# Sums of weight blocks made by adding DRAM-to-DRAM transfers, and 17 seven-product pairs for 13, in a hybrid encoder block

## The chip, the cores and the metric

The kernel runs on one core of a Trainium2 chip. The metric is the device time of one execution in microseconds. The time before is the median of three runs, 1146.89 us (1146.48 to 1147.50).

The core's engines are called by short names. PE is TensorE (matrix products; PEld is its loading of the stationary operand), DVE is VectorE, ACT is ScalarE, POOL or Pool is GpSimd, and SP is SyncE, which issues nearly all transfers. Sixteen DMA engines carry the transfers of all queues.

## The reference

One layer of an encoder block for 256 tokens of 2048 features, in float32:

```
hn   = rmsnorm(x);  proj = hn @ w_in            # (256, 2048) @ (2048, 3616)
mix  = concat(ssd_mixer(proj), pool_mixer(proj)) @ w_out
h    = x + rmsnorm(mix)
up   = rmsnorm(h) @ w_ffn_up                    # (256, 2048) @ (2048, 11264)
gate, val = split(up);  gate = gelu(dwconv3(gate))
ff   = (gate * val) @ w_ffn_down                # (256, 5632) @ (5632, 2048)
h    = h + rmsnorm(ff)
out  = h + rmsnorm(sigmoid(rmsnorm(h) @ w_ple_gate) * (p @ w_ple))
```

The change concerns the product with `w_ffn_down`, the down projection. The state-space mixer (`ssd_mixer`) matters because its small steps run on Pool.

## The kernel before

**Products.** Every float32 operand is split into a high part (rounded to float32r) and a low part (the rest), and a product is made of three: high by high, high by low, low by high. `split` (line 138) does this for weights: ACT casts the high part (line 147), DVE subtracts it (line 148). Every product is issued in `mm` (line 86), so all matrix products of the profile have the line L86 and are told apart by their tiles.

**Stages, in the order of the code.** Input projection of `dt` and the pooling inputs (`dtu`), then of the mixer's inputs in three slabs (`xbc`), then of `z` (tiles `z`); between them small steps of the mixer are put in by a list of jobs. Then the output projection (`wo`), the up product in 11 slabs of 512 gate and 512 value columns (`ga` and `va`), the down projection (`dn`), and the gate of the last embedding (`gt`). The mixer's steps on Pool that matter here: `rms` (lines 312 and 315) gives `rx`, the row scales with which DVE and ACT empty the first accumulators (lines 457 to 461); `seg_prep` (line 509) builds `ap` for the `seg` products; `weigh` (line 581) builds `w`; `far` (line 597) builds `xd` for the `yo` products, which stand among the products of `z`. In the up product Pool has one multiplication for each slab (line 767).

**Down projection.** `sublayer` (line 701) runs it in two halves of 1024 output columns. In each half `token_major` (line 240) walks through 22 pairs of weight rows: `raw` (line 151) loads a pair, 2 x 128 rows by 1024 columns (1024 KB), into one of three buffers. An ordinary pair is split and gives 24 products of 128 x 512. A fast pair goes through `seven_products` (line 201): it treats pair and column halves as a 2 x 2 matrix of blocks and needs seven block products in place of eight, 21 products in all. DVE makes the sums of weight blocks in place (lines 209 to 211), `hid_sums` (line 800) makes those of the input blocks, and `combine` (line 222) brings the accumulators together after the last fast pair. Fast are 6 of 22 pairs in the first half and 7 in the second (line 828). The input sums of the first four fast pairs are kept in two pages and used again in the second half.

**Buffers.** `page` (line 70) gives one of 13 buffers of 128 x 2048 float32; `mid` (line 73) one of three of half the size. During the up product all 13 pages are in use: six for `hid`, four for the normalised input (`wox`), two for `h`, one for `pl`.

**Order.** Each engine runs its queue strictly in the order of the built program, and an instruction waits there for the semaphores of its inputs. That order isn't the order of the code: a scheduler lays the instructions out when the program is built, by their priority, their dependencies and the buffers that are free. An instruction whose inputs are there and whose buffer is free can stand far ahead of its place in the code. Loads on SP are held by their buffers (`raw` has three), and where `load` (line 115) is told so also by the load before.

Of the kernel before, what the change touches and what calls it, by code (L numbers as in the profile page):

```python
# [51 lines left out]
def build(nc, a, out):  # L52
# [5 lines left out]
    with tile.TileContext(nc) as tc, \  # L58
            tc.tile_pool(name="const", bufs=1) as cp, \
            tc.tile_pool(name="weights", bufs=1) as wp, \  # L60
            tc.tile_pool(name="pages", bufs=1) as gp, \
            tc.tile_pool(name="small", bufs=1) as sp, \
            ExitStack() as early, \
            tc.tile_pool(name="pmain", bufs=6, space=bass.MemoryType.PSUM) as pm, \
            tc.tile_pool(name="pmisc", bufs=2, space=bass.MemoryType.PSUM) as pc:
# [44 lines left out]
        vt = cp.tile([P, V_N - V_SCW], F32, name="vt")  # L110
        small = ep.tile([P, 80 + 512], F32, name="small")

        last = {}

        def load(dst, src, ahead=False):

            with tc.issue_after(last["dma"]) if last and not ahead else nullcontext():
                return ins(nc.sync.dma_start(dst, src))
# [31 lines left out]

        def raw(name, src, a_, b_):
            r = wp.tile([P, 2048], F32, tag="raw", bufs=3, name=name)
            last["dma"] = load(r[:, :a_ * b_].rearrange("p (a b) -> p a b", a=a_), src, True)
            return r

# [42 lines left out]
                yield o, c  # L198
                c += o.shape[-1]

        def seven_products(name, r, a_, acc, alt, start, stop):

            v = r.rearrange("p (b c) -> p b c", b=4)
            b11 = split(f"{name}a", r[:, :512], 512)
            b2 = split(f"{name}b", r[:, 1024:], 1024)

            nc.vector.tensor_sub(v[:, 0:2], v[:, 1::2], v[:, 0:2])
            nc.vector.tensor_sub(v[:, 3], v[:, 3], v[:, 0])  # L210
            nc.vector.tensor_sub(v[:, 2], v[:, 2], v[:, 3])
            t13 = split(f"{name}c", r[:, :1024], 1024)
            t42 = split(f"{name}d", r[:, 1024:], 1024)
            for x, (wh, wl), c, o, own in (
                    ("a11", b11, 0, alt[0], True), ("a12", b2, 0, acc[0][0], False), ("s4", b2, 512, acc[0][1], False),
                    ("s1", t13, 0, alt[1], True), ("s3", t13, 512, alt[2], True), ("a22", t42, 0, acc[1][0], False),
                    ("s2", t42, 512, alt[3], True)):
                xh, xl = a_[x]
                for q, (xx, ww) in enumerate(((xh, wh), (xh, wl), (xl, wh))):
                    mm(o, xx, ww[:, c:c + 512], own and start and q == 0, own and stop and q == 2)  # L220

        def combine(name, acc, alt):

            m = [mid(f"{name}v{i}") for i in range(2)]
            p1, s16, s165, s167 = (m[i // 2][:, i % 2 * 512:(i % 2 + 1) * 512] for i in range(4))

            def add(o, a_, b):
                nc.vector.tensor_add(o, a_, b)

            nc.scalar.copy(p1, alt[0])  # L230
            add(s16, alt[3], p1)
            add(acc[0][0], acc[0][0], p1)
            add(s165, alt[1], s16)
            add(acc[0][1], acc[0][1], s165)
            add(s167, alt[2], s16)
            add(acc[1][0], acc[1][0], s167)
            add(s165, alt[2], s165)
            add(acc[1][1], acc[1][1], s165)

        def token_major(name, w, c0, ks, get, acc, tail=1, fast=(), alt=None, sums=None):  # L240


            group, nu = [], len(ks) // 2
            for u in range(nu):
                k0 = ks[2 * u]
                r = raw(f"{name}r{k0}", w[k0 * P:(k0 + 2) * P, c0:c0 + 1024]
                        .rearrange("(k p) c -> p k c", p=P), 2, 1024)
                if u in fast:
                    seven_products(f"{name}{k0}", r, sums(k0), acc, alt, u == fast[0], u == fast[-1])
                    continue  # L250
                for j in range(2):
                    group.append((k0 + j, *split(f"{name}{k0}_{j}", r[:, j * 1024:(j + 1) * 1024], 1024)))
                if nu - tail <= u < nu - 1:
                    continue

                order = [(t, o, g, q) for t in range(2) for o in columns(acc[t]) for g in group for q in range(3)] \
                    if u == nu - 1 or u - 1 in fast[-1:] else \
                    [(t, o, g, q) for g in group for t in range(2) for q in range(3) for o in columns(acc[t])]
                for t, (o, c), (k, wh, wl), q in order:
                    xh, xl = (v[:, t * P:(t + 1) * P] for v in get(k))  # L260
                    xx, ww = ((xh, wh), (xh, wl), (xl, wh))[q]
                    mm(o, xx, ww[:, c:c + o.shape[-1]], k == ks[0] and q == 0, k == ks[-1] and q == 2)
                if u - 1 in fast[-1:]:
                    combine(name, acc, alt)
                group = []
                aside()
# [464 lines left out]
        def ple(half):  # L731
            pl = page(f"pl{half}")
            acc = [main(f"ple{half}{t}") for t in range(2)]
            token_major(f"ple{half}", w_ple, half * 1024, [0, 1], lambda k: (pth[:, k, :], ptl[:, k, :]), acc)
            for t in range(2):
                for n in range(2):
                    nc.scalar.activation(pl[:, t * 1024 + n * 512:t * 1024 + (n + 1) * 512], acc[t][n],
                                         AF.Copy, scale=0.5)
            return pl
# [9 lines left out]
                      V_FN, Pairs)  # L749


        pl = [ple(0)]
        rf = row_rstd("rf", h)
        rfb = along_tokens("rfb", rf)
        hid = [page(f"hid{i}") for i in range(6)]
        for s in range(DFF // 512):
            sc = mid(f"gr{s}")
            for i in range(2):
                ga = main(f"ga{s}{i}")
                feature_pairs(f"ug{s}{i}", w_up, s * 512 + i * 256, hf, ga)  # L760
                o = sc[:, i * 512:(i + 1) * 512]
                total(o, ga)
                v = o.rearrange("p (f t) -> p f t", f=2)
                nc.vector.tensor_tensor(v, v, rfb.unsqueeze(1).to_broadcast([P, 2, L]), op=ALU.mult)
            cv = conv(f"fc{s}", sc, 3, V_FCW + 4 * s, NF, V_FCB + 4 * s)
            nc.scalar.activation(cv, cv, AF.Gelu_apprx_tanh)  # L766
            nc.gpsimd.tensor_tensor(cv.rearrange("p (f t) -> p f t", f=4), cv.rearrange("p (f t) -> p f t", f=4),  # L767
                                    rfb.unsqueeze(1).to_broadcast([P, 4, L]), op=ALU.mult)
            for i in range(2):
                va = main(f"va{s}{i}")  # L770
                feature_pairs(f"uv{s}{i}", w_up, DFF + s * 512 + i * 256, hf, va)
                c0 = (s % 2) * 1024 + i * 512
                hd = hid[s // 2][:, c0:c0 + 512]
                total(hd, va)
                nc.vector.tensor_mul(hd, hd, cv[:, i * 512:(i + 1) * 512])

        cur = {}

# [16 lines left out]
                hcache[k0], hcache[k0 + 1] = get_hid(k0), get_hid(k0 + 1)  # L795
            return hcache[k]

        keep, kept = [], {}

        def hid_sums(k):  # L800


            (h1, l1), (h2, l2) = get_hid(k), get_hid(k + 1)
            if k not in kept:
                src = hid[k // 8][:, (k % 8) * L:(k % 8 + 2) * L]
                a11, a21, a12, a22 = (src[:, i * P:(i + 1) * P] for i in range(4))
                n = len(kept)
                if n in (0, 2):
                    keep.append(page(f"hsum{k}", F32R))
                s = mid(f"hd{k}")  # L810
                s1, s2, s3, s4 = (s[:, i * P:(i + 1) * P] for i in range(4))
                nc.vector.tensor_add(s1, a21, a22)
                nc.vector.tensor_sub(s3, a11, a21)
                nc.vector.tensor_sub(s2, s1, a11)
                nc.vector.tensor_sub(s4, a12, s2)
                o = keep[-1][:, n % 2 * 1024:(n % 2 + 1) * 1024] if n < 4 else mid(f"he{k}", F32R)
                nc.scalar.copy(o[:, :512], s[:, :512])
                nc.vector.tensor_sub(o[:, 512:], s[:, :512], o[:, :512].bitcast(F32))
                if n < 4:
                    kept[k] = o  # L820
            else:
                o = kept[k]
            d = {f"s{i + 1}": (o[:, i * P:(i + 1) * P], o[:, 512 + i * P:512 + (i + 1) * P]) for i in range(4)}
            d.update(a11=(h1[:, :P], l1[:, :P]), a12=(h2[:, :P], l2[:, :P]), a22=(h2[:, P:], l2[:, P:]))
            return d

        hp = sublayer("dn", w_down, list(range(NF)), hid_get, gload("gffn", a["ffn_norm_post"][0]), h, V_PN,
                      fast=((2, 5, 8, 11, 14, 17), (2, 5, 8, 11, 14, 17, 19)), sums=hid_sums)


        pl.append(ple(1))
# [110 lines left out]
```

## Time and profile before

| what | us |
|---|---|
| median of three runs | 1146.89 |
| profiled execution, whole time | 1147.28 |
| profiled execution, span of the profile | 1145.5 |
| PE busy | 1126.3 |
| DVE busy | 824.8 |
| ACT busy | 598.3 |
| Pool busy | 122.5 |

The DMA engines moved 219 MB, nearly all on SP's queue (q1), and HBM was written with 2.1 MB. The granted clock of TensorE was 0.994 of full speed on average. In the profile a row of 40 digits divides the span into 40 slices of 28.6 us, each digit the busy share in tenths. A row of a timeline has start, duration, engine, line, operation, output and inputs, and in brackets the idle time before it and what ended it.

### The profile page before, as it was taken

The numbers are of one execution on the slowest core, as the hardware profiler recorded it, in microseconds if no ns is written. First come the engines' busy times: TensorE is split into PE (matmuls) and PEld (weight loads), VectorE is DVE, ScalarE is ACT, GpSimd is POOL, SyncE is SP. The second block draws the span as 40 slices with busy tenths as digits, with TensorE's granted clock in tenths as the row PEclk, the third lists the DMA queues.
The fourth block names the chain that finished last, engine by engine and source line by source line (L and its number), as shares of the span: only waits on it lengthen the run. The fifth ranks groups of instructions, "written<-read, shape, count | busy, mean of one in ns | idle before, by whom it ended". The sixth has DMA issues, their size and how long they took to land.

```text
span 1145.5 us, 15408 instructions
## 1 busy us (share of the span) xinstructions
PE 1126.3 (98%) x6057; PEld 971.6 (85%) x6057; DVE 824.8 (72%) x1060; ACT 598.3 (52%) x812; POOL 122.5 (11%) x123
## 2 busy tenths in 40 slices
PE   9998999999999999999999999999999999999996
PEld 9997987888888888888888888888888888887885
DVE  6578896654777665666766766668888888898573
ACT  7533543553675454544544545545555556657462
POOL 0274504200110000000000000000000000002001
PEclk9998999999999999999999999999999999999998
DMA  9952347546365555555555565556466646564752
GB/s 358 337 184 74 111 150 267 201 156 216 121 213 186 192 192 195 190 185 184 184 187 193 181 207 189 184 184 221 159 209 221 204 163 221 187 206 159 226 179 74
DMA packets 129592, 219.03 MB, mean 191 GB/s; under 512 B 3696, under 2 KB 96752, under 8 KB 128624
## 3 DMA queue, kind: packets, MB, share of 16 engines
q1 hardware_dynamic: 129232, 217.70, 57.4%
q8 instruction: 47, 0.77, 0.3%
q10 hardware_dynamic: 288, 0.36, 0.1%
q14 instruction: 25, 0.20, 0.1%
HBM read 215.95 MB, written 2.10 MB: 190 GB/s over the span
## 4 chain that ended last, share of the span: by engine, by line
PE 92%; DVE 5%; POOL 1%; ACT 1%; issue 1%; POOLq 0%; DVEq 0%; ACTq 0%
PE va L86 21%; PE ga L86 21%; PE dna L86 17%; PE woa L86 8%; PE gt L86 7%; PE dtu L86 4%; PE z L86 4%; PE xbc L86 3%; PE dns L86 3%; DVE cv L373 2%; DVE w L586 1%; DVE xb_0l L148 1%; PE ple L86 1%; PE yd L86 0%; DVE h L726 0%
## 5 line engine op out<-in xcount | busy, mean ns | idle before, releaser
L86 PE MATMUL ga<-wox,ug_0h 128*128 128x512 f32 x352 | 125.5, 395 | 0.0
L86 PE MATMUL ga<-wox,ug_1h 128*128 128x512 f32 x352 | 125.1, 394 | 0.0
L86 PE MATMUL va<-wox,uv_0h 128*128 128x512 f32 x352 | 124.8, 393 | 0.0
L86 PE MATMUL va<-wox,uv_1h 128*128 128x512 f32 x352 | 124.8, 393 | 0.0
L86 PE MATMUL ga<-wox,ug_0l 128*128 128x256 f32 x352 | 99.1, 282 | 0.0
L86 PE MATMUL ga<-wox,ug_1l 128*128 128x256 f32 x352 | 99.1, 282 | 0.0
L86 PE MATMUL va<-wox,uv_0l 128*128 128x256 f32 x352 | 99.1, 281 | 0.0
L86 PE MATMUL va<-wox,uv_1l 128*128 128x256 f32 x352 | 99.1, 281 | 0.0
L86 PEld LDWEIGHTS va<-wox,uv_0h 128*128 128x128 f32 x352 | 66.1, 188 | 15.0
L86 PEld LDWEIGHTS va<-wox,uv_1h 128*128 128x128 f32 x352 | 66.1, 188 | 15.0
L86 PEld LDWEIGHTS ga<-wox,ug_1h 128*128 128x128 f32 x352 | 66.1, 188 | 14.9
L86 PEld LDWEIGHTS ga<-wox,ug_0h 128*128 128x128 f32 x352 | 66.1, 188 | 14.8
L86 PE MATMUL dna<-dn_0h,hs 128*128 128x512 f32 x248 | 75.8, 393 | 0.0
L86 PE MATMUL dna<-dn_1h,hs 128*128 128x512 f32 x248 | 75.6, 393 | 0.0
L767 POOL TENSOR_TENSOR fc<-fc,rfb 128x1024 f32<-128x1024 f32 x11 | 26.4, 2404 | 440.2 <-ACT fc L766 440.2
L86 PEld LDWEIGHTS ga<-wox,ug_0l 128*128 128x128 f32 x352 | 66.2, 188 | 0.1
L86 PEld LDWEIGHTS ga<-wox,ug_1l 128*128 128x128 f32 x352 | 66.2, 188 | 0.0
L86 PEld LDWEIGHTS va<-wox,uv_0l 128*128 128x128 f32 x352 | 66.2, 188 | 0.0
L86 PEld LDWEIGHTS va<-wox,uv_1l 128*128 128x128 f32 x352 | 66.2, 188 | 0.0
L86 PEld LDWEIGHTS dna<-dn_1h,hs 128*128 128x128 f32 x248 | 46.5, 188 | 10.8
L86 PEld LDWEIGHTS dna<-dn_0h,hs 128*128 128x128 f32 x248 | 46.5, 188 | 10.7
L86 PE MATMUL dna<-dn_0l,hs 128*128 128x512 f32 x124 | 40.2, 393 | 0.0
(1075 smaller groups left out, 2860.3 us busy)
## 6 DMA issues: line engine op xcount, KB each, us to landing
dn0r<-w_ffn_down SPq DMA_DIRECT2D x22, 1024.0 KB, 5.5
dn1r<-w_ffn_down SPq DMA_DIRECT2D x22, 1024.0 KB, 5.5
zr<-w_in SPq DMA_DIRECT2D x8, 1024.0 KB, 5.2
wo0r<-w_out SPq DMA_DIRECT2D x8, 1024.0 KB, 5.6
wo1r<-w_out SPq DMA_DIRECT2D x8, 1024.0 KB, 5.5
gt0r<-w_ple_gate SPq DMA_DIRECT2D x8, 1024.0 KB, 6.0
gt1r<-w_ple_gate SPq DMA_DIRECT2D x8, 1024.0 KB, 5.6
dtur<-w_in SPq DMA_DIRECT2D x14, 528.0 KB, 8.6
```

The lines of the kernel that those rows point to most:

```text
L86: nc.tensor.matmul(o, lhsT, rhs, start=start, stop=stop, skip_group_check=True)
L148: last["dve"] = ins(nc.vector.tensor_sub(lo[:, s], src[:, s], hi[:, s].bitcast(F32)))
L373: nc.vector.scalar_tensor_tensor(o[:, lo:hi], i[:, lo + d:hi + d], vec(wcol + j * wstep + f), o[:, lo:hi], op0=ALU.mult, op1=ALU.add)
L586: nc.vector.scalar_tensor_tensor(w[:, h * P:(h + 1) * P], cbm[:, 0, g, t, :], dt[:, t, 8 * g + h:8 * g + h + 1], w[:, h * P:(h + 1) * P], ...
L767: nc.gpsimd.tensor_tensor(cv.rearrange("p (f t) -> p f t", f=4), cv.rearrange("p (f t) -> p f t", f=4), rfb.unsqueeze(1).to_broadcast([P, ...
```

## The change

The sums of weight blocks are no longer made by DVE. For each fast pair a DRAM tile of 128 x 2048 float32 is added, and Pool issues four transfers from DRAM to DRAM that fill it: a copy of the pair's four blocks (1024 KB); an adding transfer that adds the right-hand blocks to the first two (1024 KB); and two adding transfers within the tile (512 KB each). Each waits for the one before it. The code issues them in the loop of the up product, twice in each slab, four in one place for four different pairs. The signs of the sums change, and so `hid_sums` and `combine` change some additions to subtractions.

`seven_products` loads 768 KB of the unchanged blocks into a `raw` buffer with two transfers, and the 1024 KB of sums into a page with a third. The kept input sums and their two pages go, so `hid_sums` makes every pair's sums afresh. Fast pairs are now (2, 4, 7, 9, 12, 14, 17, 19) and (2, 4, 6, 8, 11, 13, 15, 17, 19): 17 for 13.

```diff
+        def block_sums(name, w, which):
+            jobs = []
+            def step(c0, k, i):
+                t = sums_[c0, k]
+                v = t.rearrange("p (b c) -> p b c", b=4)
+                if i == 0:
+                    nc.gpsimd.dma_start(t.rearrange("p (k c) -> p k c", k=2),
+                                        w[k * P:(k + 2) * P, c0:c0 + 1024].rearrange("(k p) c -> p k c", p=P))
+                elif i == 1:
+                    nc.gpsimd.dma_start(v[:, 0:2], w[k * P:(k + 2) * P, c0 + 512:c0 + 1024]
+                                        .rearrange("(k p) c -> p k c", p=P), accum_op=ALU.add)
+                elif i == 2:
+                    nc.gpsimd.dma_start(v[:, 3], v[:, 0], accum_op=ALU.add)
+                else:
+                    nc.gpsimd.dma_start(v[:, 2], v[:, 3], accum_op=ALU.add)
+            for c0, k in which:
+                sums_[c0, k] = dp.tile([P, 2048], F32, tag=f"bs{c0}_{k}", bufs=1, name=f"{name}{c0}_{k}")
+            for j in range(len(which) + 3):
+                jobs.append([lambda a_=(*which[j - i], i): step(*a_) for i in (3, 2, 1, 0) if 0 <= j - i < len(which)])
+            return jobs
...
-        def seven_products(name, r, a_, acc, alt, start, stop):
-            v = r.rearrange("p (b c) -> p b c", b=4)
+        def seven_products(name, w, k0, c0, a_, acc, alt, start, stop):
+            r = raw(f"{name}r", None, 0, 0)
+            last["dma"] = load(r[:, 512:1536], w[(k0 + 1) * P:(k0 + 2) * P, c0:c0 + 1024], True)
+            last["dma"] = load(r[:, :512], w[k0 * P:(k0 + 1) * P, c0:c0 + 512], True)
+            t = page(f"{name}t")
+            last["dma"] = load(t, sums_[c0, k0], True)
             b11 = split(f"{name}a", r[:, :512], 512)
-            b2 = split(f"{name}b", r[:, 1024:], 1024)
-            nc.vector.tensor_sub(v[:, 0:2], v[:, 1::2], v[:, 0:2])
-            nc.vector.tensor_sub(v[:, 3], v[:, 3], v[:, 0])
-            nc.vector.tensor_sub(v[:, 2], v[:, 2], v[:, 3])
-            t13 = split(f"{name}c", r[:, :1024], 1024)
-            t42 = split(f"{name}d", r[:, 1024:], 1024)
+            b2 = split(f"{name}b", r[:, 512:1536], 1024)
+            t13 = split(f"{name}c", t[:, :1024], 1024)
+            t42 = split(f"{name}d", t[:, 1024:], 1024)
...
+        dn_fast = (2, 4, 7, 9, 12, 14, 17, 19), (2, 4, 6, 8, 11, 13, 15, 17, 19)
+        ahead = block_sums("bs", w_down, [(c * 1024, 2 * u) for c, f in enumerate(dn_fast) for u in f])
...
+            for job_ in (ahead.pop(0) if ahead else ()):
+                job_()
             cv = conv(f"fc{s}", sc, 3, V_FCW + 4 * s, NF, V_FCB + 4 * s)
...
                 nc.vector.tensor_mul(hd, hd, cv[:, i * 512:(i + 1) * 512])
+            for job_ in (ahead.pop(0) if ahead else ()):
+                job_()
```

More of the change, by code (lines that the diff above doesn't have):

```diff
@@ L62, in build @@
             tc.tile_pool(name="small", bufs=1) as sp, \
+            tc.tile_pool(name="dram", bufs=1, space=bass.MemoryType.DRAM) as dp, \
             ExitStack() as early, \
@@ L111, in build @@
         small = ep.tile([P, 80 + 512], F32, name="small")
-        last = {}
+        last, sums_ = {}, {}
         def load(dst, src, ahead=False):
@@ L152, in raw @@
             r = wp.tile([P, 2048], F32, tag="raw", bufs=3, name=name)
+            if src is None:
+                return r
             last["dma"] = load(r[:, :a_ * b_].rearrange("p (a b) -> p a b", a=a_), src, True)
@@ L225, in combine @@
             p1, s16, s165, s167 = (m[i // 2][:, i % 2 * 512:(i % 2 + 1) * 512] for i in range(4))
-            def add(o, a_, b):
-                nc.vector.tensor_add(o, a_, b)
+            add, sub = nc.vector.tensor_add, nc.vector.tensor_sub
             nc.scalar.copy(p1, alt[0])
-            add(s16, alt[3], p1)
+            sub(s16, p1, alt[3])
             add(acc[0][0], acc[0][0], p1)
             add(s165, alt[1], s16)
-            add(acc[0][1], acc[0][1], s165)
+            sub(acc[0][1], acc[0][1], s165)
             add(s167, alt[2], s16)
@@ L237, in combine @@
             add(s165, alt[2], s165)
-            add(acc[1][1], acc[1][1], s165)
+            sub(acc[1][1], acc[1][1], s165)
         def token_major(name, w, c0, ks, get, acc, tail=1, fast=(), alt=None, sums=None):
@@ L245, in token_major @@
                 k0 = ks[2 * u]
+                if u in fast:
+                    seven_products(f"{name}{k0}", w, k0, c0, sums(k0), acc, alt, u == fast[0], u == fast[-1])
+                    continue
                 r = raw(f"{name}r{k0}", w[k0 * P:(k0 + 2) * P, c0:c0 + 1024]
                         .rearrange("(k p) c -> p k c", p=P), 2, 1024)
-                if u in fast:
-                    seven_products(f"{name}{k0}", r, sums(k0), acc, alt, u == fast[0], u == fast[-1])
-                    continue
                 for j in range(2):
@@ L796, in hid_get @@
             return hcache[k]
-        keep, kept = [], {}
         def hid_sums(k):
             (h1, l1), (h2, l2) = get_hid(k), get_hid(k + 1)
[L804 to L822, printed above, removed]
+            src = hid[k // 8][:, (k % 8) * L:(k % 8 + 2) * L]
+            a11, a21, a12, a22 = (src[:, i * P:(i + 1) * P] for i in range(4))
+            s, o = mid(f"hd{k}"), mid(f"he{k}", F32R)
+            s1, s2, s3, s4 = (s[:, i * P:(i + 1) * P] for i in range(4))
+            nc.vector.tensor_sub(s1, a22, a21)
+            nc.vector.tensor_sub(s3, a11, a21)
+            nc.vector.tensor_add(s2, s1, a11)
+            nc.vector.tensor_sub(s4, a12, s2)
+            nc.scalar.copy(o[:, :512], s[:, :512])
+            nc.vector.tensor_sub(o[:, 512:], s[:, :512], o[:, :512].bitcast(F32))
             d = {f"s{i + 1}": (o[:, i * P:(i + 1) * P], o[:, 512 + i * P:512 + (i + 1) * P]) for i in range(4)}
@@ L825, in hid_sums @@
             return d
+        assert not ahead
         hp = sublayer("dn", w_down, list(range(NF)), hid_get, gload("gffn", a["ffn_norm_post"][0]), h, V_PN,
-                      fast=((2, 5, 8, 11, 14, 17), (2, 5, 8, 11, 14, 17, 19)), sums=hid_sums)
+                      fast=dn_fast, sums=hid_sums)
         pl.append(ple(1))
```

## The prediction, made before the changed kernel ran

> **What bounds the kernel now.** I read the page's head first, then the busy time by stretch, then the chain that ended last, and last Pool's timeline, because the change puts its new work on Pool.
>
> ```profile
> span 1145.5 us, 15408 instructions
> PE 1126.3 (98%) x6057; PEld 971.6 (85%) x6057; DVE 824.8 (72%) x1060; ACT 598.3 (52%) x812; POOL 122.5 (11%) x123
> ...
> POOL 0274504200110000000000000000000000002001
> ...
> q1 hardware_dynamic: 129232, 217.70, 57.4%
> ```
>
> PE is busy nearly throughout, Pool (busy tenths in 40 slices) works mostly in the first quarter, and the DMA engines look nearly half free: SP's queue took 57.4% of them. The stretches say the same in numbers (columns: stretch, length, busy time of PE, PEld, DVE, ACT, POOL, clock, DMA share, GB/s):
>
> ```profile
> 0.00:57.30 57.30, 55.90 (x348) 55.11 (x349) 35.45 (x54) 37.25 (x54) 8.55 (x16) 1.00 0.93 348
> 57.30:172.00 114.70, 108.63 (x744) 100.82 (x744) 98.57 (x158) 48.39 (x67) 49.83 (x38) 0.97 0.40 130
> ...
> 805.00:1033.00 228.00, 228.00 (x989) 185.26 (x988) 197.83 (x234) 135.63 (x169) 0.90 (x2) 1.00 0.59 195
> ```
>
> In the down projection (the third row) PE has no gap at all, so only fewer products shorten it. In the first row the 16 DMA engines are full: 348 GB/s at a share of 0.93 is 374 GB/s for engines that are never idle, so that one pass over 1024 KB (1.049 MB) takes 2.80 us of all 16.
>
> **The products.** A pair of weight rows takes 24 products the ordinary way and 21 in `seven_products`. Four more pairs are fast, which is 12 products fewer. Their pace is in the chain:
>
> ```profile
> 849.06 11.11 PE dna L86 x48
> ```
>
> 11.11 / 48 = 0.231 us, and 12 x 0.231 = **2.8 us off**.
>
> The stage's loads and casts (the issues: count, KB of each, us to landing; then the group of a cast):
>
> ```profile
> dn0r<-w_ffn_down SPq DMA_DIRECT2D x22, 1024.0 KB, 5.5
> dn1r<-w_ffn_down SPq DMA_DIRECT2D x22, 1024.0 KB, 5.5
> ```
>
> ```profile
> L147 ACT CAST dn_1h<-dn1r 128x1024 fp32r<-128x1024 f32 x15 | 15.7, 1049 | 1.2 <-PE dna L86 1.2
> ```
>
> Beside these products and not on the path: DVE loses L209 to L211 in 13 pairs, and gains eight more sets of input sums (nothing is kept any more) and the casts of four more fast pairs. This lies under PE, which has no gap in 228 us while DVE is busy for 197.83. What SP loads grows from 44 times 1024 KB to 27 x 1 + 17 x 1.75 = 56.75 times: 12.75 x 2.80 = 36 us more of the DMA engines, 0.59 to 0.75 of the stage, hidden as well. The first load of sums takes a page that the up product gives back at its end; behind it stand the other SP loads. Two ordinary pairs (11.1 us of PE) cover its 5.5 us and four casts of 1.05 us; without that cover it would cost up to 9.7 us, once.
>
> **Where the transfers stand.** The code writes them between the slabs of the up product, but nothing there holds them: their inputs are weights in DRAM, and each sum has a buffer of its own. The scheduler decides, and the profile shows what it does with an instruction without inputs:
>
> ```profile
> 0.89 0.11 POOL half_up L841
> ```
>
> Line 841 stands behind the whole down projection, and it ran at 0.89 us. The built program of the changed kernel has Pool's queue so (position in the queue, new line numbers; A is the first pair, Z the last):
>
> ```
> 8    L213 copy A             11  L216 add A  [waits for copy A]
> 13   L219 add A [waits]      16  L221 add A  [waits]
> 32   L337 rx0m               55  L534 first ap
> 120  L219 add Z [waits]      121 L606 w
> 122  L221 add Z [waits]      125 L622 first xd
> ```
>
> All 68 transfers stand in positions 8 to 122, ahead of `xd` and interleaved with the small operations of the front. Each add waits on Pool for the transfer before it, and whatever is behind it in the queue waits too. In the kernel before, these operations ran at:
>
> ```profile
> 38.03 0.19 POOL L312 TENSOR_SCALAR rx0m<-rxq 128x1 f32<-128x1 f32 x1 [5.11 <-ACT rxj L338]
> 64.54 1.07 POOL L509 TENSOR_TENSOR ap<-dah,small 128x512 fp32r<-128x512 f32 x1 [20.71 <-DVE dah L484]
> 177.38 1.96 POOL L597 TENSOR_TENSOR xd<-xs,dec 128x1024 f32<-128x1024 f32 x1 [33.27 <-ACT xs L565]
> 186.50 1.02 PE L86 MATMUL yo<-xd,cbm 128*128 128x512 f32 x2
> ```
>
> PE needs them in its own fixed order: the first accumulators are emptied with `rx` (and are wanted for the next product), the `seg` products read `ap`, and `yo` at 186.5 reads `xd`. So PE stops at each until Pool is there, and the time at which Pool reaches `xd` moves everything behind it. PE's lost clock after such stops costs nothing more: Pool stays behind, not PE.
>
> **The price.** No adding transfer and no copy from DRAM to DRAM is in this trace. Per pair there are four: 1024 KB copied, 1024 KB added, twice 512 KB added. In units of one pass over 1024 KB:
> - one pass for each byte that lands: 1 + 1 + 0.5 + 0.5 = 3, or 8.4 us;
> - all that is read (an add reads source and destination): 1 + 2 + 1 + 1 = 5, or 14.0 us;
> - every read and every write: 2 + 3 + 1.5 + 1.5 = 8, or 22.4 us;
> - the last, and no overlap between transfers: 4 times 5.5 - 2.8 = 2.7 us more, 33.2 us.
>
> The only stores to DRAM in this trace are the eight of the output, 256 KB each (shortest, median and longest time to landing):
>
> ```profile
> DMA to landing us min/median/max: 2.5/2.7/2.8
> ```
>
> A load of that size would take about 2.7 + 2.8 / 4 = 3.4 us, an estimate from the load's 5.5.
> So a written pass costs no more than a read one, but whether it costs anything beside the read isn't shown. I take the middle between reads alone and both, 18.2 us a pair, 17 x 18.2 = 309 us. The same engines carry the loads of the front up to `xd`: 0.93 x 57.3 + 0.40 x 114.7 = 99 us. For stretches in which Pool computes and no transfer is under way I take 15 us, between none and Pool's own 8.55 + 49.83 = 58 us there. Pool reaches `xd` at 309 + 99 + 15 = 423 instead of 177: **246 us late**.
>
> The Trainium skill, "DMA: Bandwidth & Descriptors", section "Latency and other measured facts", has 214 GB/s for copies between HBM tensors at full rate; no run here shows that yet. If the 3 x 1.049 MB a pair landed at this rate, it would be an estimate of 14.7 us a pair and some 1331 us in all.
>
> **Sum.** The profiled execution took 1147.28 us (1145.5 in the span, 1.8 around it), 0.4 over the median of 1146.89. 1147.3 + 246 - 2.8 = **1390 us**.
>
> **Rivals.**
> 1. *The order does no harm, and the products are all that is left*: 1147.3 - 2.8 = 1144.5 us. That needs Pool at `xd` by 177: (177 - 99) / 17 = 4.6 us a pair even with no idle time at all, 0.68 TB/s of landed bytes from engines that were full at 0.374. That is the point where the sign turns. The half-empty DMA engines speak for it, the waits on Pool against it. Chance 0.03. The Trainium skill, the same page, section "Rules for kernel authors", says to issue a DMA early, to compute, and to wait late; here the issue is early, and the wait is early too.
> 2. *Contention alone*: Pool isn't held up, but the full front shares its engines half and half: 0.93 x 57.3 = 53 us, 1198 us. Against it: the same waits. Chance 0.05.
> 3. *One pass for each landed byte*: 17 x 8.4 + 99 + 15 - 177 = 80, so 1225 us. The read and the write side would have to run beside each other, with the second operand free. Chance 0.08.
> 4. *Only reads count*: 17 x 14.0 + 99 + 15 - 177 = 175, so 1319 us. For it: the stores' landing time. Chance 0.22. The Trainium skill, "Collectives: The Full Stack", section "The bandwidth ceiling: the fold count and why AG ≠ RS ≠ AR", puts an add's price in its two reads on the one read ring, not in the arithmetic, which is this case; no run here shows it yet.
> 5. *No overlap, or an add that is slow in itself*: 17 x 33.2 + 99 + 15 - 177 = 501, so 1646 us. For it: each add waits for the one before it, and Pool issues in order. Against it: two or three pairs are always interleaved in the queue. Chance 0.17.
>
> That the sums aren't made during the up product, as the change says, is part of the forecast.
>
> **How the numbers follow.** The forecast has 0.45; with the rivals 0.03, 0.05, 0.08, 0.22 and 0.17 that is 1. Likeliest is 1390. From 1220 to 1640 the range holds the forecast, rivals 3 and 4 and nearly half of rival 5; rivals 1 and 2 and the slow tail stay out, under 2 in 10. It is wide because one price, the pair's, moves the time by 17 us for each us. About 0.2% (2.3 us) can be told from no change here. Only rival 1 isn't slower: 2.8 us is 0.24%, so faster 0.02, same 0.01, slower 0.97.
>
> **What would show it.** Pool's timeline: `rx0m` some 100 us late, the first `ap` past 180, the first `xd` near 423, and transfers in DMA queue rows that weren't there. PE's row with low digits over the first third, the DMA row at 9 there. From the up product on the stages as before, the stage of the down projection 2.8 us shorter at the same pace, without waits for `t`. I am wrong if the adds are still running beside the up product, if `xd` is at 177, or if PE's gaps lie in the down projection.

## The result, and the profile after

The changed kernel took **1288.36 us** (median of four runs, 1286.78 to 1289.35), where the kernel before took 1147.2 us beside it: a ratio of 1.123 with an interval of 1.1216 to 1.1243, or 141 us more. The prediction was 1390 us with a range from 1220 to 1640. The profiled execution took 1289.1 us, 1.8 of it outside the span.

One correction comes first. The adding transfers are half as large as the description of the change and the prediction have them: a pair has a copy of 1024 KB, an add of 512 KB and two of 256 KB, as the profile's table of transfers after the change shows (count, KB each, median time to landing). The last two rows are loads of the front:

```profile
bs<-w_ffn_down POOLq DMA_DIRECT2D x17, 1024.0 KB, 14.2
...
bs<-w_ffn_down POOLq DMA_DIRECT2D x17, 512.0 KB, 11.3
bs<-bs POOLq DMA_DIRECT2D x34, 256.0 KB, 9.7
...
dtur<-w_in SPq DMA_DIRECT2D x14, 528.0 KB, 21.7
xb2r<-w_in SPq DMA_DIRECT2D x4, 1024.0 KB, 33.9
```

In the kernel before, the same two loads landed after 8.6 and 10.6 us:

```profile
dtur<-w_in SPq DMA_DIRECT2D x14, 528.0 KB, 8.6
xb2r<-w_in SPq DMA_DIRECT2D x4, 1024.0 KB, 10.6
```

The head of the page after, the two rows of digits and the queues:

```profile
span 1287.3 us, 15602 instructions
...
PE 1147.6 (89%) x6045; PEld 986.8 (77%) x6045; DVE 821.8 (64%) x1069; ACT 608.3 (47%) x828; POOL 176.2 (14%) x191
...
PE   7826366539999999999999999999999999999997
...
POOL 2223465530500000000000000000000000001001
...
q0 software_dynamic: 14144, 35.66, 14.0%
```

PE's digits are low in the first nine slices (about 290 us) and 9 from there on: the loss lies in the front. Queue q0, which Pool's transfers use, is new: 14.0% of 1287.3 us is **180 us** of all 16 engines, or 10.6 us a pair. The stretches (length, busy time of PE, PEld, DVE, ACT and POOL, clock, DMA share, GB/s):

```profile
0.00:57.30 57.30, 43.82 (x218) 38.58 (x219) 22.38 (x33) 21.71 (x34) 12.30 (x21) 0.94 1.00 292
57.30:172.00 114.70, 48.60 (x283) 45.98 (x282) 42.26 (x46) 21.61 (x25) 43.83 (x53) 0.70 0.96 250
172.00:250.00 78.00, 59.44 (x398) 56.27 (x397) 43.06 (x73) 27.29 (x42) 40.02 (x37) 0.85 1.01 209
250.00:320.00 70.00, 40.63 (x220) 35.56 (x221) 40.60 (x62) 19.46 (x25) 16.13 (x17) 0.78 0.67 157
943.00:1169.00 226.00, 226.00 (x982) 183.71 (x981) 188.31 (x256) 146.45 (x189) 0.64 (x2) 1.00 0.75 255
```

The DMA engines are full for 250 us, where before they were full for 57 and at 0.40 for the next 115. In the second row PE has fallen from 108.63 to 48.60 us of work. The last row is the down projection: no gap in PE, DMA at 0.75. Pool's timeline after:

```profile
92.72 0.19 POOL L337 TENSOR_SCALAR rx0m<-rxq 128x1 f32<-128x1 f32 x1
...
151.93 1.81 POOL L534 TENSOR_TENSOR ap<-dah,small 128x512 fp32r<-128x512 f32 x1
...
275.58 2.18 POOL L606 TENSOR_TENSOR w<-cbm,dt 128x1024 f32<-128x1024 f32 x1
279.95 0.83 POOL L221 DMA_DIRECT2D bs<-bs  x1 [2.19 <-DMA bs<-bs]
...
319.93 1.96 POOL L622 TENSOR_TENSOR xd<-xs,dec 128x1024 f32<-128x1024 f32 x1 [33.11 <-ACT xs L590]
```

The second `w` comes at 275.58 us and the last transfer is issued at 279.95. The second `w` of the kernel before:

```profile
132.93 2.75 POOL L581 TENSOR_TENSOR w<-cbm,dt 128x1024 f32<-128x1024 f32 x1 [7.89 <-DVE cv L373]
```

There Pool had been idle for 7.89 us and DVE ended the wait; after, the row has no idle time ahead of it. `w` is 142.65 us late, and `xd` is 142.55 us late with the same idle time ahead of it, 33.11 us for 33.27, put down to ACT both times. So **on the chain that ended last, the second `w` is the last operation that the transfers hold**, and `xd` only follows. (A third `w`, at 280.51, stands behind the last transfer of all and is 143.24 us late, but it isn't on that chain.) The waits after say who hands it on (total, times, longest):

```profile
POOL bs L221 <- DMA bs<-bs: 70.0, 12, 12.0
...
POOL bs L216 <- DMA bs<-w_ffn_down: 55.0, 13, 8.8
DVE w L611 <- POOL w L606: 52.7, 2, 28.6
```

Pool waits for its own transfers, DVE for Pool.

### The profile page after: what moved, and what is told of

Its sections match the earlier page's. It is cut to its first block, busy times and chain, and to the rows that moved or that the text cites. A ratio compares the mean times of both kernels' runs of the same rounds, so it can differ in the third digit from the quotient of the medians.

```text
span 1287.3 us, 15602 instructions
## 1 busy us (share of the span) xinstructions
PE 1147.6 (89%) x6045; PEld 986.8 (77%) x6045; DVE 821.8 (64%) x1069; ACT 608.3 (47%) x828; POOL 176.2 (14%) x191
## 3 DMA queue, kind: packets, MB, share of 16 engines
q1 hardware_dynamic: 131952, 231.07, 53.9%
q0 software_dynamic: 14144, 35.66, 14.0%
## 4 chain that ended last, share of the span: by engine, by line
PE 75%; DMA 15%; POOL 5%; issue 3%; DVE 1%; ACT 1%; POOLq 0%; DVEq 0%; ACTq 0%
PE va L87 19%; PE ga L87 19%; PE dna L87 14%; DMA bs<-w_ffn_down 13%; PE woa L87 7%; PE gt L87 6%; PE dns L87 4%; PE z L87 3%; DMA bs<-bs 3%; POOL ap L534 2%; PE xbc L87 1%; PE ple L87 0%; PE yd L87 0%; POOL bs L216 0%; POOL bs L219 0%
## 5 line engine op out<-in xcount | busy, mean ns | idle before, releaser
L87 PE MATMUL dna<-dn_0h,hs 128*128 128x512 f32 x216 | 66.5, 393 | 0.0
L87 PE MATMUL dna<-dn_1h,hs 128*128 128x512 f32 x216 | 66.3, 393 | 0.0
L87 PEld LDWEIGHTS dna<-dn_1h,hs 128*128 128x128 f32 x216 | 40.5, 188 | 9.4
L87 PEld LDWEIGHTS dna<-dn_0h,hs 128*128 128x128 f32 x216 | 40.5, 188 | 9.3
L611 DVE SCALAR_TENSOR_TENSOR w<-cbm,dt,w 128x128 f32<-128x128 f32 x32 | 12.8, 466 | 52.7 <-POOL w L606 52.7
```

The source lines that it names most:

```text
L87: nc.tensor.matmul(o, lhsT, rhs, start=start, stop=stop, skip_group_check=True)
L611: nc.vector.scalar_tensor_tensor(w[:, h * P:(h + 1) * P], cbm[:, 0, g, t, :], dt[:, t, 8 * g + h:8 * g + h + 1], w[:, h * P:(h + 1) * P], ...
```

## The experiments

The kernels below ran beside the kernel before (medians of 1147.0 to 1147.4 us). Three theories were weighed: Pool's queue hands the lateness on (the prediction), contention for the DMA engines alone does, or the transfers are too much work wherever they stand. Intervals are given where there are several runs; the other kernels have a single run, and only differences of ten us and more are read from these.

**1. The transfers held back to the up product.** The order is written down: each group of transfers waits for the multiplication of the slab before it.

```diff
+            last["pool"] = ins(nc.gpsimd.tensor_tensor(r, m, mhalf[:, :n], op=ALU.pow))
...
+            last["pool"] = ins(nc.gpsimd.tensor_tensor(cv..., rfb..., op=ALU.mult))
...
+                with tc.issue_after(last["pool"]):
+                    job_()
```

> The same 68 transfers, but each held behind the Pool multiplication of the slab before it, so that they run beside the up product. Theory A (Pool's queue: the front lost its time because small Pool operations stood behind transfers that wait): the front is as before the change, the first rx at 38, xd at 177, and what is left is 12 products fewer: 1144 to 1147 us. Theory B (the DMA engines: 180 us of transfers cost about what they cost, wherever they stand): the up product, whose loads fill 0.58 of the engines, grows by tens of us, 1170 to 1250.

It took 1212.67 us, a ratio of 1.0577 (1.0561 to 1.0593). The front is as in the kernel before, so the place was worth 76 us; but 65 us are lost in the up product. Its stretch and two loads of one slab:

```profile
420.00:840.00 420.00, 377.85 (x2055) 326.24 (x2054) 236.38 (x297) 178.83 (x240) 67.00 (x62) 0.94 0.89 234
```

```profile
ug20r<-w_ffn_up SPq DMA_DIRECT2D x2, 1024.0 KB, 7.3
ug21r<-w_ffn_up SPq DMA_DIRECT2D x2, 1024.0 KB, 22.9
```

PE stood still for 42 of 420 us there, at a clock of 0.94 (which by an estimate, 0.06 x 378, is another 23 us), although the engines still had 11% to spare on average. Up to four transfers went off together behind each multiplication, and the loads behind them landed after 23 us instead of 5 to 7. The waits show PE behind ACT's cast, and the cast behind such a load:

```profile
PE ga L87 <- ACT ug_0h L148: 38.3, 8, 7.8
...
ACT ug_0h L148 <- DMA ug71r<-w_ffn_up: 21.9, 2, 12.4
```

Holding the transfers back is not enough; they came in bursts.

**2. No transfers.** The page gets weight rows in place of the sums, with the same bytes and products; the sums are left out.

```diff
-            last["dma"] = load(t, sums_[c0, k0], True)
+            last["dma"] = load(t.rearrange("p (k c) -> p k c", k=2), w[k0 * P:(k0 + 2) * P, c0:c0 + 1024]...)
```

> No transfers at all: the page of sums is loaded from the weights themselves, so the sums are left out and the output is another one; 17 fast pairs, all else as in the changed kernel. Both theories: the front as before and 12 products of 0.231 us fewer, 1144.4 us, if the two additional loads and the page cost nothing; above 1147 if they do. Its distance to the held kernel is what the transfers cost beside the up product: 0 by theory A, tens of us by B.

1145.28 us, a ratio of 0.9983 (0.9974 to 0.9991). That is what the rest of the change is worth: 2.0 us off, between 1.0 and 3.0. The down projection is as full and as well covered as after the change:

```profile
805.00:1033.00 228.00, 228.00 (x989) 185.46 (x988) 191.37 (x258) 148.32 (x193) 2.15 (x7) 1.00 0.75 248
```

So all 143 us between 1145.28 and 1288.36 are the transfers'.

**3. The chain without its bytes.** The same 68 transfers with the same waits, 32 columns wide; the sums are left out.

> The chain of waits without the bytes: the same four dependent transfers for each of 17 pairs where the scheduler puts them, but each of 32 columns, some 3% of the bytes; the page of sums is loaded from the weights, so the sums are left out. If the bytes set the delay (17 times the engine time of a pair): what is left is 68 issues of about 0.9 us on Pool and fixed landing times, rx some 20 to 50 us late, 1165 to 1200 us. If waits as such set it (8 to 10 us each whatever the size): near 1288.

1182.72 us, 37 more than without transfers. The queue's row and `xd`:

```profile
q0 software_dynamic: 7888, 1.40, 1.6%
```

```profile
213.59 1.96 POOL L622 TENSOR_TENSOR xd<-xs,dec 128x1024 f32<-128x1024 f32 x1 [33.11 <-ACT xs L590]
```

With 1.40 MB instead of 35.66 `xd` is still 36 us late. The waits of Pool for its transfers (total, times, longest):

```profile
POOL bs L218 <- DMA bs<-w_ffn_down: 12.0, 6, 5.7
...
POOL bs L220 <- DMA bs<-bs: 10.9, 7, 2.6
...
POOL bs L216 <- DMA bs<-w_ffn_down: 3.4, 1, 3.4
```

Pool stands still for its transfers 14 times, 26 us in all, and beside that it has 68 of them to issue. The chain that ended last goes through these transfers and their issues up to 79 us, so Pool's queue is the path here. Whether it makes the 37 us alone isn't shown: even these small transfers take 1.6% of 1180.9 = 19 us of the engines, in a front whose loads already fill them for 57 us.

**4. Copies for adds.** The three adds become plain copies of the same places; the sums are left out.

```diff
-  nc.gpsimd.dma_start(v[:, 3], v[:, 0], accum_op=ALU.add)
+  nc.gpsimd.dma_start(v[:, 3], v[:, 0])
```

> The same chain and the same landed bytes, each add replaced by a plain copy, so the sums are wrong by what the adds add. If a second read is what an add costs (three reads a pair for two landed units): engine time of the transfers 180 to about 120 to 145 us, so some 35 to 60 us off the changed kernel, 1228 to 1253. If only landed bytes count: 1288 as before.

1239.55 us, 49 less than the changed kernel.

```profile
q0 software_dynamic: 9792, 35.66, 10.0%
```

The same 35.66 MB land with 10.0% of 1237.8 = 124 us of engine time instead of 180. Adding in place of copying costs 56 us of engine time, a third of the 180.

**5. The transfers alone.** Nothing is computed: four rounds of single transfers with a wait after each, and then the 17 chains.

> Only transfers, nothing of the block is computed: first four times in a row, each waiting for the one before it, a copy of 1024 KB, a copy of 512 KB, an add of 512 KB, a copy of 256 KB and an add of 256 KB; then the 17 pairs' chains as in the changed kernel, with the engines free. If a pair's price is engine time (180 us for 17 in the changed kernel): the chains take 150 to 190 us alone. If most of it was sharing with the front's loads: well under 120 us. If an add costs its second read: the add of 512 KB lands about 1.4 us after the copy of 512 KB; if it is slow in itself, several us later.

Pool's timeline of the first round shows each transfer from one issue to the next: copy 1024 KB, copy 512, add 512, copy 256, add 256.

```profile
1.30 0.83 POOL L91 DMA_DIRECT2D one<-w_ffn_down  x1 [0.86 <-PEq L56]
7.45 0.74 POOL L92 DMA_DIRECT2D one<-w_ffn_down  x1 [5.32 <-DMA one<-w_ffn_down]
12.06 1.17 POOL L93 DMA_DIRECT2D one<-w_ffn_down  x1 [3.87 <-DMA one<-w_ffn_down]
19.79 0.57 POOL L94 DMA_DIRECT2D one<-one  x1 [6.56 <-DMA one<-w_ffn_down]
23.79 0.83 POOL L95 DMA_DIRECT2D one<-one  x1 [3.43 <-DMA one<-one]
28.75 0.69 POOL L91 DMA_DIRECT2D one<-w_ffn_down  x1 [4.12 <-DMA one<-one]
```

The copies take 6.2, 4.6 and 4.0 us, the adds 7.7 and 5.0. A second read would by itself add 1.4 us at 512 KB and 0.7 at 256, estimates from the 2.80 us of a pass; the adds take 3.1 and 1.0 us more than the copies. So alone an add costs more than its second read, and why stays open. The 17 chains behind the rounds ran from 111.6 to 324:

```profile
111.60:324.00 212.40, 61.14 (x70) 1.00 0.94 183
```

That is 212 us at a DMA share of 0.94, 12.5 us a pair, and longer than the 150 to 190 us expected. The engines were busy for 0.94 x 212.4 = 200 us (two single copies of 1024 KB at the start of this stretch included). So alone, too, the chains nearly fill the engines, and the 180 us of the changed kernel are real work and not a result of crowding.

**6. The sums on DVE.** The kernel before with the 17 fast pairs, and DVE making the sums as it did; no transfers.

> The kernel before with the 17 fast pairs of the changed one, the sums still made by DVE; no transfers. If DVE's slack in the down projection (198 of 228 us) covers them: 1144 to 1145 us, and the transfers weren't needed. If not: a fast pair costs DVE some 8 to 9.5 us against 4.85 us of PE, an ordinary one 3.1 against 5.5; over a half that is 120 to 122 us against 116, so 10 to 15 us slower, 1155 to 1160.

1150.71 us, a ratio of 1.0029 (1.0018 to 1.0039). The down projection:

```profile
805.00:1033.00 228.00, 225.66 (x973) 181.66 (x971) 217.56 (x280) 142.58 (x182) 0.84 (x2) 1.00 0.57 191
```

DVE comes to 217.56 of 228 us, and PE has gaps of 2.3. The loss is smaller than expected, but with the sums on DVE the 12 products fewer don't pay.

**7. Bytes without waits.** Seven plain copies of 5120 KB at the front, none of which waits for another, in place of the chains; the sums are left out.

```diff
+        for k in range(7):
+            t = dp.tile([P, 10240], F32, tag=f"bulk{k}", bufs=1, name=f"bulk{k}")
+            nc.gpsimd.dma_start(t.rearrange("p (k c) -> p k c", k=5),
+                                w_down[k * 640:(k + 1) * 640, :].rearrange("(k p) c -> p k c", p=P))
```

> Engines loaded, Pool not held: in place of the chains seven plain copies within DRAM, 36.7 MB in all, as much as the chains land, from the same place at the front, with no wait between them; the page of sums is loaded from the weights, so the sums are left out. Against the run of chained copies (1239.6, 124 us of engine time): if sharing the engines alone makes the loss, as much, 1225 to 1245. If Pool's waits add to it: the front loses up to the 53 us in which its loads need full engines, 1175 to 1200, and rx stays near 40 to 60.

1256.07 us, which is more than either theory had expected. The queue, the first two stretches and Pool's `rx0m`:

```profile
q0 software_dynamic: 4592, 36.70, 7.9%
```

```profile
0.00:57.30 57.30, 26.58 (x106) 24.18 (x106) 12.11 (x21) 12.86 (x23) 3.50 (x10) 0.75 0.97 360
57.30:172.00 114.70, 61.96 (x376) 60.72 (x377) 29.64 (x31) 29.86 (x34) 5.94 (x10) 0.74 0.96 346
```

```profile
82.89 0.19 POOL L338 TENSOR_SCALAR rx0m<-rxq 128x1 f32<-128x1 f32 x1 [78.50 <-ACT rxj L364]
```

Pool is idle for 78.50 us ahead of `rx0m` and waits for ACT's data: its queue isn't what is late. The engines worked 0.97 x 57.3 + 0.96 x 114.7 = 166 us up to 172. If the copies' 99 us lie in there (their last issue is at 111, and the share after 172 is 0.26), the loads got 67 us of it, 40%, for the 99 us that they had there before. Contention alone costs 111 us here over experiment 2. Why that is some 12 us more than the copies' own engine time wasn't followed further.

**8. The transfers spread.** One or two at each of 44 points of the up product, each behind a tiny copy on Pool that reads the half slab which DVE has just finished.

```diff
+        def pace(src):
+            mark = tiny("mark", 1)
+            with tc.issue_after(ins(nc.gpsimd.tensor_copy(mark, src[:, 0:1]))):
+                for job_ in ahead.pop(0):
+                    job_()
...
+                pace(o)
...
+                pace(hd)
```

> The held kernel with the transfers spread evenly: one or two at each of 44 points of the up product, each behind a Pool copy of one column that waits for that point. The loads fill 0.58 of 485 us, the transfers need some 180 us more, so 0.95 on average. If the held kernel lost its 65 us to bursts (four transfers at once behind each slab's multiplication, loads landing in 20 us where the three buffers cover 11): 1145 to 1165. If the engine time itself is too much beside the loads: 1195 to 1215 as held.

**1145.18 us**, a ratio of 0.9982 (0.9972 to 0.9991): 2.2 us less than the kernel before beside it, and less than the changed kernel by 143.

```profile
q0 software_dynamic: 14144, 35.66, 15.8%
```

```profile
320.00:805.00 485.00, 484.58 (x2772) 425.07 (x2773) 327.52 (x412) 244.45 (x325) 101.97 (x126) 1.00 0.97 268
```

The transfers take the same 181 us of the engines (15.8% of 1142.8), the share is 0.97 for 485 us, and PE loses nothing. The loads of this stage mostly land after 8 to 11 us, and no group's median is over 15.2; with bursts it was up to 24.8.

**9 and 10. Nothing of the front on Pool.** The chains stay at the front of Pool's queue, but DVE does what Pool did there (`rx`, `ap`, `dec`, `w`, `xd` and others); the power in the row scales is left out. Beside it a control with the same move and no transfers.

```diff
-                nc.gpsimd.tensor_tensor(ap_[:, j], src[:, t, hs]...
+                nc.vector.tensor_tensor(ap_[:, j], src[:, t, hs]...
...
-            nc.gpsimd.tensor_tensor(w.rearrange("p (h l) -> p h l", h=8),
+            nc.vector.tensor_tensor(w.rearrange("p (h l) -> p h l", h=8),
```

> All 68 transfers stay at the front of Pool's queue with their waits, but the small operations of the front (rx, aneg, ap, dec, w, xd, y, rz) are done by DVE, so that nothing in the front waits for Pool any more. Left out: the power in the row scales (each is set to 1). In the changed kernel the transfers kept the engines busy for 180 us and cost 143 us. If Pool's queue is what hands the lateness on, the loads alone are left: the three kernels with bytes and waits show 14.0% x 1287 = 180 us of engine time, and 7 bulk copies of 99 us without waits cost 109 us. Theory Q (the queue adds to contention, since each of the small operations stands behind transfers that can end only later): about 1190 to 1240, clearly under the changed kernel. Theory C (at the front contention alone sets it, and the waits on Pool are in its shadow): 1265 to 1295, as the changed kernel. What DVE does in Pool's place is some 58 us at most, which the control without transfers shows.

> Control: the same move of the front's small operations from Pool to DVE, and no transfers at all (the sums are left out, the weight rows are loaded in their place, and the power in the row scales is left out). Without transfers and without the move it took 1145.3. DVE has room in the front (35 of 57 us and 99 of 115 us busy in the kernel before), so 1145 to 1165. The difference between the two kernels of this pair is what the transfers cost when nothing waits for Pool.

1267.26 us with the transfers and 1159.02 without: **108 us** that no wait on Pool hands on. The chain that ended last shows it; the first longer pieces for the changed kernel (start, length):

```profile
1.36 9.82 DMA bs<-w_ffn_down
12.25 15.20 DMA bs<-w_ffn_down
27.73 13.40 DMA bs<-w_ffn_down
41.41 13.30 DMA bs<-bs
```

and with the front's operations on DVE:

```profile
2.58 9.60 DMA dtur<-w_in
12.20 18.74 DMA xt<-x_cols
30.96 24.19 DMA dtur<-w_in
55.17 32.92 DMA pt<-p_t
```

The first goes from transfer to transfer, the second from load to load. Taken away, the queue leaves a path through late loads that is three quarters as costly.

The differences fit together: 37 us for the queue nearly without bytes (experiment 3), 108 for the bytes without the queue (9 and 10), 145 in sum, and 143 for both together. That these two simply add isn't shown: they are single runs of kernels whose order differs, and the 37 hold some contention too. What is shown is that most of the loss is left when the queue is taken away.

## Why the prediction was right or wrong

**What bounds the kernel.** Right: PE from the up product on, full DMA engines in the front, and no cover for a stall there.

**The products.** 2.8 us were predicted, and experiment 2 shows 2.0, with 2.8 inside its interval. What was costed at nothing there (DVE's casts, 12.75 more units of loads, the page of the first sums) did cost nothing that shows; the DMA share was predicted at 0.75 and is 0.75.

**Where the transfers stand.** Right: they ran at the front, not beside the up product, because nothing held them. The size of the lateness was too large at each place: `rx0m` was 55 us late (about 100 predicted), the first `ap` came at 152 (past 180), `xd` at 320 (423).

**The price of a pair: the step that failed.** It took 18.2 us and the trace shows 10.6, which is 17 x 7.6 = 129 us too much. The bounds were built on the wrong sizes. With 512 and 256 KB for the adds, one pass for all that is read is 1 + 1 + 0.5 + 0.5 = 3 units or 8.4 us, every stream 5 units or 14.0, and the middle that the prediction chose 11.2. The same sum with 11.2 gives 190 + 99 + 15 - 177 = 127, or 1272 us. That 11.2 comes near 10.6 is partly luck: the middle stands for half a price of the written side, and experiment 7 shows none. The sizes stand in the slices of the code (two blocks of 128 x 512 float32 are 512 KB).

**The rest of that sum.** It looked at `xd`, and the last held operation was `w`, 44 us earlier in the kernel before. Put there, it has 180 us for the transfers and 0.93 x 57.3 + 0.40 x 75.6 = 83.5 us for the loads up to 132.9; 12 us are left to reach 275.6, where 15 were taken for idle time. 1147.3 + 142.65 - 2.8 = 1287.2 us, against 1289.1 of the profiled execution. The form of the sum (all the work on the 16 engines until Pool is through) stands. Its two errors had opposite signs: with the measured 10.6 us a pair and still at `xd`, it gives 180 + 99 + 15 - 177 = 117, or 1262 us, 27 too few. So the 1390 was nearer than its price deserved, and the width of the range did the rest.

**Its reason stands only in part.** The prediction put the delay down to Pool's queue and gave contention alone 53 us (rival 2), by halving the first 57 us. Without Pool's queue the loss is 108 us: the loads get less than half (40% in experiment 7, by the sum given there), and for as long as the transfers last. Pool's waits are the path in the changed kernel, but by these single runs they add only some 35 of the 143 us.

**The rivals.** The first, no harm, comes true only where the transfers are spread (experiment 8); at the front 10.6 us a pair is over twice the 4.6 at which its sign would have turned. The third's price, a pass for each landed byte, would be 2 units or 5.6 us with the right sizes, and fails. The fourth, that only reads count, is closest: 8.4 us by its rule against 10.6. Experiment 7 has it at its cleanest: 36.70 MB copied in 99 us, 371 GB/s, for 374 of plain loads, so that the written side costs nothing beside the read. From copies to adds the reads grow from 2 units to 3, by 1.5, and the engine time from 124 to 180, by 1.45. But the packets of queue q0 grow as well, from 9792 to 14144, by 1.44, for the same landed bytes, so the second reads and the smaller packets aren't told apart by these runs. Both times lie above the price of plain loads for what they read (95 and 143 us) by 30 and 26%. What that surcharge is stays open; the packets could be it, which hold some 8.0 KB each in experiment 7 and 3.6 and 2.5 KB here, but no run changes them alone. The fifth, no overlap, had 33.2 us a pair, or 24.8 with the right sizes, and fails.

**Rates and rules drawn on.** The Trainium skill, "Collectives: The Full Stack", section "The bandwidth ceiling: the fold count and why AG ≠ RS ≠ AR", puts an add's price in its two reads; 1.45 for 1.5 fits that, with the packets as a second reading. The Trainium skill, "DMA: Bandwidth & Descriptors", section "Latency and other measured facts", has 214 GB/s for the copies between HBM tensors that it measured. Landed bytes moved here at 198 GB/s in the chains with adds (35.66 MB in 180 us), at 288 in the chains of copies, and at 371 in plain copies of 5120 KB, so 214 is no ceiling for a copy. The prediction's estimate of 14.7 us a pair from that rate rested on the wrong sizes as well; 2 x 1.049 MB would give an estimate of 9.8. The same page of the Trainium skill, section "Rules for kernel authors", says to issue a DMA early, to compute, and to wait late. Here the issue at the front, with the waits early as well, cost 141 us; with the issue spread beside the up product (experiment 8) the kernel took 2 us less than before, which is what the 12 products fewer are worth.

## What to carry to other kernels

A transfer without dependencies stands wherever the scheduler puts it, and here that was the front; if it should run beside a later stage, tie it to that stage's progress, a little at a time. What it costs is not its engine time but how late it makes the loads that a stage is waiting for, and the work that stands behind it in its own queue: the same 180 us cost 141 us at the front, 65 in bursts and nothing when spread, so compare the landing time of the loads with what their buffers cover. And take the size of each transfer from the code's slices before pricing it.

## What the runs showed of the hardware that was not expected

- Engines 97% busy for 485 us cost PE nothing (experiment 8), while 89% in bursts cost it 42 of 420 us (experiment 1).
- In experiment 7 Pool's queue had more than half of full engines, some 60% by the sum given there. Its packets hold some 8.0 KB and those of SP's queue 1.7 (231.07 MB in 134128), and SP's loads wait for buffers; which of these sets the share wasn't tested.
- An adding transfer alone takes 7.7 us for 512 KB where a copy takes 4.6, and 5.0 for 256 KB where a copy takes 4.0 (experiment 5).
